# A hybrid block on one core: late gates as a product of seven, sums from raw tiles, and copies and additions issued by GpSimd

## The chip, the cores and the metric

One NeuronCore of a Trainium2 chip runs the whole kernel in one launch. The metric is the device time of one execution in microseconds; the median of several runs counts. The engines: TensorE (PE, its weight loads PEld), VectorE (DVE), ScalarE (ACT), GpSimd (POOL), and SyncE (SP), which only issues DMAs here. Each engine works through its own queue in order; semaphores order engines against each other.

## The reference, cut to what matters

x has 512 tokens of 1024 features. One layer: a projection by w_in to 14,352 columns, a gated delta rule with eight heads (A), a retention with four heads (B), gates that mix both, and an MLP with 4096 hidden features. All is float32.

```python
xn = rmsnorm(x, n_mix_pre)
proj = xn @ w_in
qa, ka, va, za, beta_logit, a_dt, qb, kb, vb, gb, gate_a, gate_b = _split_cols(proj, IN_SIZES)
...
oa = chunk_gated_delta_rule(qa, ka, va, beta, g)
oa = rmsnorm(oa, norm_a) * jax.nn.silu(za.reshape(b, s, A_HEADS, A_DV))
ya = oa.reshape(b, s, A_V) @ w_br_a
...
ob = chunk_retention(qb, kb, vb)
ob = rmsnorm(ob, norm_b.reshape(B_HEADS, B_DV)) * jax.nn.silu(gb.reshape(b, s, B_HEADS, B_DV))
yb = ob.reshape(b, s, B_V) @ w_br_b
mix = (jax.nn.sigmoid(gate_a) * ya + jax.nn.sigmoid(gate_b) * yb) @ w_out
x = x + rmsnorm(mix, n_mix_post)
hn = rmsnorm(x, n_mlp_pre)
ff = jnp.square(jax.nn.relu(hn @ w_up)) @ w_down
return x + rmsnorm(ff, n_mlp_post)
```

The change touches za (2048 columns, four groups of 512 for two heads each, "gates" 0 to 3 below), vb and gb (512 columns per head), gate_a and gate_b (1024 columns each).

## The kernel before, in words

**Products.** Activations and weights are split into a high and a low part, and a product is three matmuls (high by high, high by low, low by high). A weight tile of 128x1024 floats (512 KB) is loaded by SP into one of two `raw` buffers, cast on ACT to `whi` (L145) and subtracted on DVE to `wlo` (L146); both lie in a ring of three. A raw buffer is free for the next load when the subtraction has read it.

**A product of seven.** A product of a 512x1024 activation with 1024 x 1024 weights, cut into 2 x 2 blocks each way, takes eight block products; `seven` does it in seven, from sums of blocks. The sums of the activations ("s1" to "s4") are formed on chip once, in `feature_sums`, after the second recurrence. The sums of the weights are formed in DRAM by `BlockSums`: for each of four sums two DMA copies of 512 KB (`copy`, L165, on SP's queue), and two accumulating DMAs (`add_block`, L132, on GpSimd's queue). These jobs stand in two lists, `trickle` and `later_adds`, and `pace` takes some of them behind each weight load, by a model of the queue (LOAD_US, COPY_US, ADD_US, BACKLOG) that starts at JOBS_FROM. In the two column halves c1, c2 of a unit, `seven` reads three plain blocks from w_in and four sums: 14 raw tiles. `p` and `u` are its sums of finished products.

**Stages.** The first is the delta rule: fillers (products for values `v`, queries `q`, gates `z`, and the products with w_br_a, `ya`) are laid between the steps of chains (inverse, four recurrences for two heads each, gating, transposes) by a model `Clock` that pins TensorE's order. A filler in its list has the events it waits for, such as `og2`, the gated output of heads 4 and 5. A recurrence goes over four chunks of 128 tokens; its steps on TensorE are `kf` (keys by state `st`), `qf`, `rt`, `kd` (the state's update) and `vn,dall` (the output), with short DVE or ACT operations between (L1173, L1189, L1198, L1203). Then come the retention heads and two units of 1024 columns, six uses of `seven` in all (gate a, heads 0 to 3 with vb and gb, gate b), from about 520 to 930 us; then w_out, and the MLP, whose w_down products are products of seven as well (L276 is the matmul of those).

The order of the fillers in the delta stage's last part:

```python
(gate_filler(1), ("gate0",)),
(ya_filler(1), ("og1",)),
(value_filler(3), ("og1",)),
(query_filler(3), ("og1",)),
(gate_filler(2), ("gate1",)),
(ya_filler(2), ("og2",)),
(gate_filler(3), ("gate2",)),
```

The functions that the change touches, with the line numbers of the profile:

Of the kernel before, what the change touches and what calls it, by code (L numbers as in the profile page):

```python
# [19 lines left out]
P = 128  # L20
T = 512
# [7 lines left out]
JOBS_FROM, LOAD_US, COPY_US, ADD_US, BACKLOG = 60.0, 2.0, 2.0, 3.4, 6.0  # L29
SMALL_US, CONV_US, TOK_US, PK_US, INV_US, DB_US = 10.5, 6.5, 2.5, 2.0, 46, 1.2  # L30
VT_US, KS_US, PX_US, PC_US, GATE_US, FEAT_US, INV_PRIO, CONV_PRIO, SMALL_PRIO, KEY_PRIO, DECAY_US, AHEAD, TR_US, REC_PRIO, OUT_PRIO = 2.5, 2.4, 3.5, 2.4, 11.0, 1.0, 0, 600, 800, 600, 20.0, 700, 2.2, 900, 900
# [31 lines left out]
def hybrid_block_kernel(ctx: ExitStack, tc: tile.TileContext, a: dict, out: bass.AP):  # L63
# [32 lines left out]
    def weights(src, k0, nk, c0, ncols, keep=None, paced=True):  # L96
# [9 lines left out]
        pace(load)  # L106
# [5 lines left out]
    def pace(load):  # L112

        if clocks:
            spent[0] = clocks[0].now
        if spent[0] is None:
            return
        queued[0] = max(queued[0], spent[0]) + LOAD_US
        with tc.issue_after(load.ins):
            while (trickle or later_adds) and queued[0] < spent[0] + BACKLOG:  # L120
                ready = len(later_adds) > -(-len(trickle) // 8) * 8
                if ready and (added[0] or not trickle):
                    add_block()
                    queued[0] += ADD_US
                elif trickle:
                    copy_block()
                    queued[0] += COPY_US
                added[0] = not added[0]

    def add_block():  # L130
        dst, src = later_adds.pop(0)
        tc.keep_in_program_order(nc.gpsimd.dma_start(dst, src, accum_op=ALU.add))  # L132
# [19 lines left out]
    class BlockSums:  # L152


        def __init__(self, src, c1, c2, tag):
# [4 lines left out]
            self.t = [dr.tile([P, 4, 512], F32, tag=f"{tag}{i}", name="sums", bufs=1) for i in range(4)]  # L160
            self.parts = []
            trickle.extend((self, i, k) for i in (2, 1, 3, 0) for k in (0, 2))

        def copy(self, i, k):
            nc.sync.dma_start(self.t[i][:, k : k + 2, :], self.first[i][:, k : k + 2, :])  # L165

        def adds(self):

            for i, k in ((2, 0), (1, 0), (3, 0), (2, 2), (1, 2), (3, 2), (0, 0), (0, 2)):
                src = (self.w12, self.t[2], self.w12, self.t[1])[i]  # L170
# [3 lines left out]
        def weights(self, i, ks):  # L174
            while any(job[0] is self for job in trickle):
                copy_block()
            while any(dst is t for dst, src in later_adds for t in self.parts):
                add_block()
            return block_weights(self.t[i - 1][:, 2 * ks : 2 * ks + 2, :])

    def block_weights(block):
# [4 lines left out]
        pace(load)  # L186
        return split_weights(raw, 1024, 2)

    ga_sums = BlockSums(w_in, OFF_GA, OFF_GA + 512, "ga")
    vg_sums = [BlockSums(w_in, OFF_VB + h * 512, OFF_GB + h * 512, f"vg{h}") for h in range(4)]  # L190
    gb_sums = BlockSums(w_in, OFF_GBR, OFF_GBR + 512, "gb")
    down_sums = [BlockSums(w_down[grp * D : (grp + 1) * D, :], 0, 512, f"dn{grp}") for grp in range(3)]
    for sums in [ga_sums] + vg_sums + [gb_sums] + down_sums:
        later_adds.extend(sums.adds())
# [38 lines left out]
    def seven(src, c1, c2, sums, product, temp, out):  # L233

        plain, summed = block_products(src, sums, product)
        p1, u2 = [temp("p1") for _ in range(2)], [temp("u2") for _ in range(2)]
        a = bank(psx)
        plain(a, "11", 0, c1, True)
# [4 lines left out]
        summed(b, "s2", 2, True)  # L243
        with tc.high_priority(400):
            for t in range(2):
                nc.vector.tensor_tensor(u2[t], p1[t], b[t], ALU.add)
        plain(a, "12", 1, c1, False)
        out(0, 0, a)
        c = bank(psm)
        summed(c, "s1", 1, True)  # L250
        summed(b, "s3", 3, False)
        with tc.high_priority(400):
            for t in range(2):
                nc.vector.tensor_tensor(p1[t], p1[t], b[t], ALU.add)
        out(1, 1, c, p1, ALU.subtract)
        d = bank(psx)
        summed(d, "22", 4, True)
        out(1, 0, d, p1, ALU.add)
        plain(c, "s4", 1, c2, False)
        out(0, 1, c, u2, ALU.subtract)  # L260
# [88 lines left out]
    ones = cp.tile([P, P], F32, name="ones")  # L349

# [53 lines left out]
    def two_halves(pool, name, tag, n, width):  # L404
        return Halves(n, [
            pf.tile([P, n, width], F32, tag=tag, name=name),
# [6 lines left out]
    kd = two_halves(pa, "kd", "f1", 16, P)  # L413
# [425 lines left out]

    class Rows:  # L840
# [94 lines left out]
    with delta_rule:  # L935
# [3 lines left out]
        def key_tile(h, ps, th=None):  # L939
# [3 lines left out]
            with tc.high_priority(KEY_PRIO):  # L943
                sum_squares(pt, ssks[h // 4][:, 4 * (h % 4) : 4 * (h % 4) + 4])
                nc.scalar.copy(kd[:, 4 * h : 4 * h + 4, :], pt)
# [210 lines left out]

        def recurrence(g2):
# [4 lines left out]
            for c in range(4):  # L1162
# [28 lines left out]
                if c < 3:  # L1191
                    pc = chain_bank()
                    for hh in range(2):
                        clock.matmul(pc[:, hs[hh], :], kd[:, nn[hh], :], vx[:, hs[hh], :], start=True, stop=True)
# [113 lines left out]
        for step in first_keys_filler():  # L1308
            while any(clock.ready(c[0]) <= clock.now for c in clock.chains):
# [23 lines left out]
                (gate_filler(2), ("gate1",)),  # L1333
                (ya_filler(2), ("og2",)),
                (gate_filler(3), ("gate2",)),
# [7 lines left out]
    with tc.tile_pool(name="pb", bufs=1) as pb_:  # L1343
# [11 lines left out]
        def values_and_gates(sums, c1, c2, g, out1, out2):  # L1355

            def out(th, ch, ps, u=None, op=None):
                for t in range(2):
# [6 lines left out]
                    else:  # L1365
                        nc.vector.tensor_tensor(u[t], ps[t], u[t], op)
                        out1(row, u[t])
# [16 lines left out]
        def scores(h, rows):  # L1384
# [13 lines left out]
            for i in range(4):  # L1398
# [13 lines left out]
                nc.vector.tensor_tensor(sc[:, :n2], ps[:, n - n2 : n], dec[:, :n2], ALU.mult)  # L1412
# [46 lines left out]
        def gate_unit(sums, off, gated):  # L1459

            def out(th, ch, ps, u=None, op=None):
                for t in range(2):
                    src = ps[t]
                    if u is not None:
                        src = tmp("g_s") if th and ch else u[t]
# [38 lines left out]
        def gate_b(t, half, src):  # L1504
            hs = slice(half * 512, half * 512 + 512)
            tb = gates[t // 2][:, t % 2, hs]
            nc.scalar.activation(tb, src, AF.Tanh, scale=0.5)
            m = acc_rows(t, half)
# [12 lines left out]
        for pair in (1, 0):  # L1521
            pss = [[psm.tile([P, T], F32, tag="mm", name="mm") for _ in range(2)] for _ in range(2)]
            for i in range(2):
                t = 2 * pair + i
                tt = slice(t * P, (t + 1) * P)
                for half in range(2):
# [6 lines left out]
                    nc.vector.scalar_tensor_tensor(m, m, 1.0, pss[i][half], ALU.add, ALU.mult)  # L1533
                    nc.vector.tensor_tensor(m, m, acc_rows(t, half), ALU.add)
# [289 lines left out]
```

## Time and profile before

| | |
|---|---|
| median of 3 runs | 1349.88 us (1347.24 to 1351.58) |
| profiled execution | 1347.26 us, span 1345.1 us |
| TensorE busy | 1327.4 us (99%) in 6639 matmuls |
| VectorE, ScalarE, GpSimd busy | 884.8, 634.4, 90.9 us |
| DMA | 236.78 MB, mean 176 GB/s |
| SP's queue (q1), GpSimd's queue (q0) | 43.6%, 19.8% of 16 DMA engines' span |

Line numbers (L146 and so on) are those of the kernel before. "a<-b" is an operation that writes a and reads b; a part in brackets is idle time of the engine just before it, and what ended that. An engine's busy time leaves out the issuing of DMAs on SP, and a load's time runs from its issue to its landing. TensorE's matmuls are pipelined, so a row's duration is longer than the step from one start to the next.

### The profile page before, as it was taken

How to read it: one execution, taken by the hardware profiler on the slowest of the kernel's cores; microseconds unless marked ns; L12 is line 12 of the kernel's file. 1: busy time of each engine (PE TensorE's matmuls, PEld its weight loads, DVE VectorE, ACT ScalarE, POOL GpSimd, SP SyncE). 2: the span in 40 equal slices, each digit the busy share in tenths (PEclk: the TensorE clock that was granted, in tenths of full speed). 3: DMA queues.
4: the chain of work that ended last, by engine and by line, in shares of the span. 5: the costliest groups of instructions: out<-in, count | busy, mean ns of one | idle time of the engine just before them, and what ended most of it. 6: DMA issues, size and time to landing. Idle time of an engine off the chain costs nothing.

```text
span 1345.1 us, 17540 instructions
## 1 busy us (share of the span) xinstructions
PE 1327.4 (99%) x6639; PEld 1101.2 (82%) x6639; DVE 884.8 (66%) x1515; ACT 634.4 (47%) x1118; POOL 90.9 (7%) x99
## 2 busy tenths in 40 slices
PE   9999999999999999999999999999999999999997
PEld 7888778888888877888888888888889888888886
DVE  6889867475476357777467576679684745828535
ACT  5783426553343424553443443455265746346441
POOL 2201110011101010001001000000100000000000
PEclk9999999999999999999999999999999999999999
DMA  6339987489779685899499695565814543535421
GB/s 193 128 95 244 230 191 149 101 227 207 170 187 210 166 227 161 262 309 221 139 278 194 172 258 142 166 206 173 265 67 147 162 146 110 188 98 179 131 78 63
DMA packets 114691, 236.78 MB, mean 176 GB/s; under 512 B 7398, under 2 KB 31120, under 8 KB 114096
## 3 DMA queue, kind: packets, MB, share of 16 engines
q1 hardware_dynamic: 95792, 185.10, 43.6%
q0 software_dynamic: 16496, 43.69, 19.8%
q10 hardware_dynamic: 2320, 6.89, 1.4%
q8 instruction: 52, 0.85, 0.3%
q14 instruction: 31, 0.25, 0.1%
HBM read 231.43 MB, written 79.71 MB: 231 GB/s over the span
## 4 chain that ended last, share of the span: by engine, by line
PE 86%; DVE 6%; ACT 4%; DMA 3%; issue 1%; DVEq 0%; ACTq 0%
PE mm L627 16%; PE mm L276 13%; PE dl L276 12%; PE mm L92 11%; PE mm L93 11%; PE mm L94 11%; PE dl L627 6%; DMA raw<-in_w_in_dram 2%; DVE wlo L146 1%; PE tr L356 1%; PE dl L93 1%; PE dl L94 1%; PE dl L92 1%; PE tr L636 1%; PE mm L591 1%
## 5 line engine op out<-in xcount | busy, mean ns | idle before, releaser
L146 DVE TENSOR_TENSOR wlo<-raw,whi 128x1024 fp32r<-128x1024 f32 x253 | 309.0, 1224 | 243.8 <-ACT whi L145 243.2
L145 ACT CAST whi<-raw 128x1024 fp32r<-128x1024 f32 x253 | 265.9, 1052 | 403.0 <-PE mm L93 100.1
L627 PE MATMUL mm<-actT,whi 128*128 128x512 f32 x448 | 144.3, 403 | 0.0
L276 PE MATMUL mm<-whi,xsum 128*128 128x512 f32 x384 | 121.9, 390 | 0.0
L94 PE MATMUL mm<-hn,wlo 128*128 128x512 f32 (+1 forms) x288 | 105.4, 366 | 0.0
L93 PE MATMUL mm<-hn,whi 128*128 128x512 f32 (+1 forms) x288 | 105.3, 366 | 0.0
L92 PE MATMUL mm<-hn,whi 128*128 128x512 f32 (+1 forms) x288 | 105.3, 366 | 0.0
L627 PEld LDWEIGHTS mm<-actT,whi 128*128 128x128 f32 x448 | 80.6, 188 | 15.1
L276 PE MATMUL dl<-whi,actT 128*128 128x512 f32 x288 | 91.9, 389 | 0.0
L627 PE MATMUL mm<-whi,actT 128*128 128x512 f32 x256 | 87.8, 406 | 1.1 <-DVE qf L857 1.0
L627 PE MATMUL mm<-actT,wlo 128*128 128x512 f32 x224 | 87.8, 392 | 0.0
L276 PEld LDWEIGHTS mm<-whi,xsum 128*128 128x128 f32 x384 | 72.0, 188 | 14.7
L276 PE MATMUL mm<-wlo,xsum 128*128 128x512 f32 x192 | 74.8, 390 | 0.0
L627 PE MATMUL mm<-whi,og 128*128 128x512 f32 x192 | 64.3, 402 | 0.0
L276 PEld LDWEIGHTS dl<-whi,actT 128*128 128x128 f32 x288 | 54.1, 188 | 11.2
L94 PEld LDWEIGHTS mm<-hn,wlo 128*128 128x128 f32 x288 | 54.3, 189 | 8.8
L93 PEld LDWEIGHTS mm<-hn,whi 128*128 128x128 f32 x288 | 54.3, 189 | 8.7
L92 PEld LDWEIGHTS mm<-hn,whi 128*128 128x128 f32 x288 | 54.3, 189 | 8.7
L276 PE MATMUL dl<-whi,ffq 128*128 128x512 f32 x192 | 61.1, 389 | 0.0
L132 POOL DMA_DIRECT2D sums<-sums x36 | 29.9, 830 | 443.2 <-DMA sums<-in_w_in_dram 238.7
L627 PEld LDWEIGHTS mm<-whi,actT 128*128 128x128 f32 x256 | 48.1, 188 | 11.5 <-issue 1.7
L276 PE MATMUL dl<-wlo,actT 128*128 128x512 f32 x144 | 56.0, 389 | 0.0
(372 smaller groups left out, 2789.7 us busy)
## 6 DMA issues: line engine op xcount, KB each, us to landing
raw<-in_w_in_dram SPq DMA_DIRECT2D x97, 512.0 KB, 5.5
raw<-sums SPq DMA_DIRECT2D x72, 512.0 KB, 4.1
sums<-in_w_in_dram SPq DMA_DIRECT2D x48, 512.0 KB, 8.0
sums<-sums POOLq DMA_DIRECT2D x36, 512.0 KB, 7.9
raw<-in_w_up_dram SPq DMA_DIRECT2D x36, 512.0 KB, 4.2
raw<-in_w_down_dram SPq DMA_DIRECT2D x26, 512.0 KB, 3.8
sums<-in_w_in_dram POOLq DMA_DIRECT2D x24, 512.0 KB, 10.8
sums<-in_w_down_dram SPq DMA_DIRECT2D x24, 512.0 KB, 6.9
```

What stands on the lines that cost most here:

```text
L92: nc.tensor.matmul(ps, lh, rh, start=first, stop=False)
L93: nc.tensor.matmul(ps, lh, rl, start=False, stop=False)
L94: nc.tensor.matmul(ps, ll, rh, start=False, stop=last)
L132: tc.keep_in_program_order(nc.gpsimd.dma_start(dst, src, accum_op=ALU.add))
L145: nc.scalar.copy(hi[:, :n], raw[:, :n])
L146: nc.vector.tensor_tensor(lo[:, :n], raw[:, :n], hi[:, :n], ALU.subtract)
L276: m = nc.tensor.matmul(pss[t], lhs[i // 2], rhs[i % 2], start=first and k + i == 0, stop=k + i == 5, skip_group_check=not first,)
L356: nc.tensor.transpose(ps, src, ident)
L591: pin(nc.tensor.matmul(first_keys[f][:, 256:512], ws[w][:, kk, :], xs[x][:, 2 * j + kk, 256:512], start=False, stop=kk == 1 and i == 2, sk ...
L627: m = tc.keep_in_program_order(nc.tensor.matmul(*args, **kwargs))
L636: tc.keep_in_program_order(nc.tensor.transpose(ps, src, ident if by is None else by))
```

## The change

1. `late_gates_filler` takes the place of `gate_filler(2)` and `gate_filler(3)`: gates 2 and 3 (1024 columns of za) are formed by a product of seven, in 14 tiles of 12 matmuls where eight tiles of 24 stood, with a new `z_sums`. It stands where gate 2 stood in the list, so both gates lie ahead of the third w_br_a product and of the last recurrence.
2. In `seven`, two of the four weight sums (the second and the fourth) are no longer made in DRAM but by `plus` on DVE from raw tiles that lie in SBUF. A unit loads ten tiles, adds four times and splits 14 tiles as before; the products come in another order (11, s3, s2, 12, 22, s1, s4), with two more additions to `p` and `u`.
3. The copies for the sums go from SP's queue to GpSimd's. Before it issues jobs, GpSimd copies one element of the weight tile that has just been loaded (`token`), so that it stands behind that landing; then up to two jobs follow, by another pace. JOBS_FROM goes from 60 to 100. There are 56 copies and 56 additions instead of 72 and 72.
4. Smaller things: the keys' token-major tiles `kd` are kept for three chunks instead of four; the decay of the scores gets a higher priority; for half of gate b's rows two DVE operations move behind the product with w_br_b.

The core of the diff:

```diff
-JOBS_FROM, LOAD_US, COPY_US, ADD_US, BACKLOG = 60.0, 2.0, 2.0, 3.4, 6.0
+JOBS_FROM, COPY_US, ADD_US = 100.0, 5.5, 7.5
...
-    def pace(load):
+    def pace(raw):
...
-        queued[0] = max(queued[0], spent[0]) + LOAD_US
-        with tc.issue_after(load.ins):
-            while (trickle or later_adds) and queued[0] < spent[0] + BACKLOG:
-                ready = len(later_adds) > -(-len(trickle) // 8) * 8
...
+        if spent[0] < queued[0] or not (trickle or later_adds):
+            return
+        tc.keep_in_program_order(nc.gpsimd.tensor_copy(token, raw[0:1, 0:1]))
+        done = 0
+        while (trickle or later_adds) and queued[0] <= spent[0] and done < 2:
+            ready = bool(later_adds) and not any(job[0] is later_adds[0][2] for job in trickle)
+            added[0] = ready and (not added[0] or not trickle)
+            if added[0]:
+                add_block()
+            else:
+                copy_block()
+            queued[0] += ADD_US if added[0] else COPY_US
+            done += 1
...
         def copy(self, i, k):
-            nc.sync.dma_start(self.t[i][:, k : k + 2, :], self.first[i][:, k : k + 2, :])
+            tc.keep_in_program_order(
+                nc.gpsimd.dma_start(self.t[i][:, k : k + 2, :], self.first[i][:, k : k + 2, :])
+            )
...
+    z_sums = BlockSums(w_in, OFF_ZA + 1024, OFF_ZA + 1536, "z")
+    ga_sums = BlockSums(w_in, OFF_GA, OFF_GA + 512, "ga", False)
...
     def seven(src, c1, c2, sums, product, temp, out):
...
+        def plus(dst, other):
+            with tc.high_priority(SUM_PRIO):
+                nc.vector.tensor_tensor(dst, other, dst, ALU.add)
...
+        x, y = raws(sums.first_raw, 1), raws(sums.raw, 3)
         a = bank(psx)
-        plain(a, "11", 0, c1, True)
+        times(a, "11", x, True)
...
-        summed(b, "s2", 2, True)
+        x = times(b, "s3", y, True, added(y, x, sums.first_raw, 3))
...
-        plain(a, "12", 1, c1, False)
+        c = bank(psm)
+        times(c, "s2", y, True)
...
+        y = times(a, "12", x, False, added(x, y, sums.raw, 1))
         out(0, 0, a)
-        c = bank(psm)
-        summed(c, "s1", 1, True)
-        summed(b, "s3", 3, False)
...
+        d = bank(psm)
+        x = times(d, "22", x, True, lambda ks: sums.first_raw(2, ks))
+        out(1, 0, d, u3, ALU.add)
+        c = bank(psm)
+        times(c, "s1", y, True)
...
+        def late_gates_filler():
...
+            yield from product(a, "11", None, True)
...
+            yield from product(b, "s2", 2, True)
...
+            yield from product(a, "12", None, False)
+            silu(0, 0, a)
+            yield from product(b, "s3", 3, False)
...
+            yield from product(c, "s1", 1, True)
...
+            yield from product(d, "22", 4, True)
...
+            yield from product(c, "s4", None, False, OFF_ZA + 1536)
...
-                (gate_filler(2), ("gate1",)),
+                (late_gates_filler, ("gate1",)),
                 (ya_filler(2), ("og2",)),
-                (gate_filler(3), ("gate2",)),
```

TensorE's order in the last recurrence before, from the third chunk's `kf` step to its `rt` step (`mm<-whi,actT` and `mm<-wlo,actT` are matmuls of gate 3):

```order
L627 MATMUL dl<-st,kf 128x256 x2
L627 MATMUL dl<-st,qf 128x256 x2
L627 MATMUL mm<-whi,actT 128x512
L627 MATMUL mm<-wlo,actT 128x512
L627 MATMUL mm<-whi,actT 128x512 x2
L627 MATMUL mm<-wlo,actT 128x512
L627 MATMUL mm<-whi,actT 128x512 x2
L627 MATMUL mm<-wlo,actT 128x512
L627 MATMUL mm<-whi,actT 128x512 x2
L627 MATMUL mm<-wlo,actT 128x512
L627 MATMUL mm<-whi,actT 128x512
L627 MATMUL dl<-vt,rt 128x256 x2
```

And now, from the first chunk's `kd` step on (L670 is the matmul of L627; L92 to L94 with `mm<-actT` belong to the next stage's query features):

```order
L670 MATMUL dl<-vt,kd 128x256 x2
L670 MATMUL dl<-vn,dall 128x256 x2
L670 MATMUL dl<-st,kf 128x256 x2
L670 MATMUL dl<-st,qf 128x256 x2
L92 MATMUL mm<-actT,whi 128x512
L93 MATMUL mm<-actT,whi 128x512
L94 MATMUL mm<-actT,wlo 128x512
L670 MATMUL dl<-vt,rt 128x256 x2
L92 MATMUL mm<-actT,whi 128x512
L93 MATMUL mm<-actT,whi 128x512
L94 MATMUL mm<-actT,wlo 128x512
L670 MATMUL dl<-vt,kd 128x256 x2
```

Twelve matmuls of gate 3 stood between two steps of the chain; three matmuls of the next stage stand there now.

DVE's order in a head's unit before (L246 and L254 are the additions to `u` and `p`, L1429 a retention operation):

```order
L146 TENSOR_TENSOR wlo<-raw,whi 128x1024 x7
L246 TENSOR_TENSOR u_5761<-p_5759,mm 128x512
L246 TENSOR_TENSOR u_5762<-p_5760,mm 128x512
L146 TENSOR_TENSOR wlo<-raw,whi 128x1024 x2
L1429 TENSOR_TENSOR vr<-dl,vr 128x512
L146 TENSOR_TENSOR wlo<-raw,whi 128x1024
L1429 TENSOR_TENSOR vr<-dl,vr 128x512
L146 TENSOR_TENSOR wlo<-raw,whi 128x1024 x3
L254 TENSOR_TENSOR p_5759<-p_5759,mm 128x512
L254 TENSOR_TENSOR p_5760<-p_5760,mm 128x512
```

The same unit now (L148 is the split of L146, L258 the addition of two raw tiles, L282 to L288 the additions to `u` and `p`):

```order
L148 TENSOR_TENSOR wlo<-raw,whi 128x1024 x2
L282 TENSOR_TENSOR u_5833<-p_5831,mm 128x512
L282 TENSOR_TENSOR u_5834<-p_5832,mm 128x512
L148 TENSOR_TENSOR wlo<-raw,whi 128x1024
L258 TENSOR_TENSOR raw<-raw 128x1024
L148 TENSOR_TENSOR wlo<-raw,whi 128x1024
L287 TENSOR_TENSOR p_5831<-p_5831,mm 128x512
L288 TENSOR_TENSOR u_5833<-u_5833,mm 128x512
L287 TENSOR_TENSOR p_5832<-p_5832,mm 128x512
L288 TENSOR_TENSOR u_5834<-u_5834,mm 128x512
L258 TENSOR_TENSOR raw<-raw 128x1024
L148 TENSOR_TENSOR wlo<-raw,whi 128x1024 x2
```

Between splits that followed each other, additions of raw tiles stand now, and four additions to `p` and `u` in a row where two stood.

GpSimd's order where the jobs begin, before:

```order
L132 DMA sums<-in_w_in_dram 128x2x512
L132 DMA sums<-sums 128x1024 x2
L132 DMA sums<-in_w_in_dram 128x2x512
L132 DMA sums<-sums 128x1024 x2
L132 DMA sums<-in_w_in_dram 128x2x512 x3
```

And now, a little after the start of the jobs (L120 is the token, L169 a copy, L134 an addition):

```order
L120 COPY token<-raw 1x1
L134 DMA sums<-in_w_in_dram 128x2x512
L120 COPY token<-raw 1x1
L169 DMA sums<-in_w_in_dram 128x2x512
L134 DMA sums<-sums 128x1024
L120 COPY token<-raw 1x1
L169 DMA sums<-in_w_in_dram 128x2x512
L134 DMA sums<-sums 128x1024
```

GpSimd's queue held additions alone; now each group of one or two jobs has a token in front, which waits for the landing of a weight tile and which that tile's buffer waits for.

176 lines of the change are left out of this document (131 added, 45 removed).

## The prediction

> **What bounds the kernel now.** I read the page first, then the stage table, the chain of waits, and TensorE's timeline around its idle places. The page's row of engines, and rows of the stage table (stretch, length, busy time of PE, PEld, DVE, ACT and POOL with their instructions, granted clock, DMA share, GB/s):
>
> ```profile
> PE 1327.4 (99%) x6639; PEld 1101.2 (82%) x6639; DVE 884.8 (66%) x1515; ACT 634.4 (47%) x1118; POOL 90.9 (7%) x99
> 300.00:400.00 100.00, 98.48 (x456) 81.34 (x455) 57.82 (x92) 42.42 (x76) 9.89 (x10) 1.00 0.81 189
> 400.00:480.00 80.00, 79.54 (x372) 65.80 (x371) 41.13 (x78) 32.41 (x73) 9.95 (x10) 1.00 0.79 188
> 480.00:520.00 40.00, 38.36 (x175) 31.02 (x174) 25.99 (x40) 11.13 (x14) 2.82 (x3) 1.00 0.81 210
> 520.00:930.00 410.00, 409.93 (x1865) 339.56 (x1864) 279.66 (x392) 185.31 (x252) 21.86 (x22) 1.00 0.75 210
> sum 1345.10, PE 1327.37 PEld 1101.17 DVE 884.84 ACT 634.37 POOL 90.91; mean PE 110.61 PEld 91.76 DVE 73.74 ACT 52.86 POOL 7.58
> ```
>
> TensorE is the bound: it idles 1345.10 − 1327.37 = 17.7 us in all. Through the retention heads and the gate units around them (520 to 930) it idles 0.07 us in 410; in the last part of the delta stage (300 to 520) 1.52 + 0.46 + 1.64 = 3.6 us. So time is won only by taking matmuls away, or out of those 3.6 us, and is lost wherever another engine or a load makes TensorE wait. The price of a 512-column matmul comes from the chain of waits (start, duration, 24 matmuls):
>
> ```profile
> 529.56 5.44 PE mm L276 x24
> ```
>
> 5.44 / 24 = 0.2267 us.
>
> **The change part by part.**
>
> *Matmuls.* The two late gates are eight weight tiles of 24 matmuls, 192 in all; as a product of seven they are 14 tiles of 12, 168. 24 × 0.2267 = **−5.44 us**, all on the bound. The six other units (gate a, four heads, gate b) were products of seven already; their matmuls only change places.
>
> *The last recurrence without its filler.* Gate 3's 96 matmuls lay between its steps. Now both late gates stand earlier, and this recurrence has six matmuls of the w_br_a product and some fifteen of the next stage's query features to cover its waits. Its steps as TensorE, ACT and DVE ran them, an earlier recurrence standing for some (start, duration, engine, line):
>
> ```profile
> 433.04 1.02 PE L627 MATMUL dl<-vt,rt 128*128 128x256 f32 x4
> 434.10 0.84 ACT L1189 ACTIVATE vt<-dl,brd 128x256 f32<-128x256 f32 x2 [1.17 <-PE dl L627]
> 438.03 1.02 PE L627 MATMUL dl<-vt,kd 128*128 128x256 f32 x4
> 438.89 1.03 PE L627 MATMUL dl<-vn,dall 128*128 128x256 f32 x4
> 439.09 0.69 DVE L1203 COPY st<-dl 128x512 f32<-128x512 f32 x1 [1.22 <-PE dl L627]
> 456.40 1.02 PE L627 MATMUL dl<-st,kf 128*128 128x256 f32 x4
> 457.47 0.88 DVE L1173 SCALAR_TENSOR_TENSOR vt<-dl,neg_eg,vt 128x256 f32<-128x256 f32 x2 [2.84 <-PE dl L627]
> 466.72 1.03 PE L627 MATMUL dl<-vn,dall 128*128 128x256 f32 x4
> 467.39 0.58 PE L92 MATMUL mm<-actT,whi 128*128 128x512 f32 x1
> 467.89 1.13 PE L627 MATMUL dl<-st,kf 128*128 128x256 f32 x4
> ```
>
> The shortest way from one step to the next is from its start to the end of the operation behind it: rt 434.10 + 0.84 − 433.04 = 1.90, kd 1.75 (1.95 where the state update has L1173's 0.88), kf 1.95. A group of four takes TensorE 438.89 − 438.03 = 0.86, so each hop leaves 0.9 to 1.1 us. The new order fills it behind kf with the qf group (0.86), behind kd with the vn,dall group and a matmul (1.09), behind rt with three matmuls (0.68). Short by 0.1, 0 and 0.3 us: four chunks come to about **+1.0**, an estimate. The row of before that is nearest to it is the hop from 466.72 to 467.89, which has the new fillers already: 467.89 − 466.72 − 0.86 − 0.23 = 0.08 idle. Ends: 0, and 4 us (1 us a chunk, where a split stands ahead of a step's copy). Two stalls follow:
>
> ```profile
> 478.69 0.33 PE L636 MATMUL tr<-cmat,vt 128*128 128x128 f32 x1 [0.46 <-DVE vt L1241]
> 511.88 0.50 PE L93 MATMUL dl<-wlo,og 128*128 128x512 f32 x1 [1.44 <-DVE wlo L146]
> ```
>
> Ahead of the transposes at 478.69 stand 26 feature matmuls now, 21 before: 5 × 0.2267 covers the 0.46, **−0.5**. The stall at 511.88 is the first tile of the last w_br_a product. Seven matmuls fewer stand ahead of it (7 × 0.2267 = 1.6), but its loads meet fewer copies: **0**, from −1.4 to +1.6.
>
> *The late gates' supply.* Splits (count, busy us, mean ns), and loads and jobs (count, KB, median us to landing), the first two of 300 to 480, the third of 520 to 930, the rest of the page:
>
> ```profile
> L146 DVE TENSOR_TENSOR wlo<-raw,whi 128x1024 fp32r<-128x1024 f32 x253 | 309.0, 1224 | 243.8 <-ACT whi L145 243.2
> L145 ACT CAST whi<-raw 128x1024 fp32r<-128x1024 f32 x253 | 265.9, 1052 | 403.0 <-PE mm L93 100.1
> raw<-in_w_in_dram SPq DMA_DIRECT2D x16, 512.0 KB, 5.7
> raw<-in_w_br_a_dram SPq DMA_DIRECT2D x10, 512.0 KB, 6.7
> raw<-in_w_br_b_dram SPq DMA_DIRECT2D x16, 512.0 KB, 8.4
> raw<-sums SPq DMA_DIRECT2D x72, 512.0 KB, 4.1
> sums<-in_w_in_dram SPq DMA_DIRECT2D x48, 512.0 KB, 8.0
> sums<-in_w_in_dram POOLq DMA_DIRECT2D x24, 512.0 KB, 10.8
> ```
>
> A raw buffer turns over in landing, cast and subtraction: 4.1 to 5.7, + 1.05 + 1.22 + about 0.2 = 6.6 to 8.2 us for two tiles, as there are two buffers. Two tiles are 2 × 12 × 0.2267 = 5.44 us of gate work, with the chain groups between them some 6.3 to 7.9, an estimate. That is a balance, and up to three split tiles wait in the ring: **0**. Engine time is there: six more splits are 7.3 us on DVE and 6.3 on ACT, which were busy 41.13 and 32.41 of 80.
>
> *The six units' sums on DVE.* A unit loads ten tiles instead of 14 and forms the other four by additions of two raw tiles on DVE: L146's shape, 1.22 us each. One unit before (its stretch of the stage table, and groups in it):
>
> ```profile
> 656.50:694.60 38.10, 38.10 (x169) 31.55 (x169) 24.61 (x27) 19.58 (x23) 1.97 (x2) 1.00 0.81 239
> L146 DVE TENSOR_TENSOR wlo<-raw,whi 128x1024 fp32r<-128x1024 f32 x14 | 17.1, 1225 | 16.5 <-ACT whi L145 16.5
> L254 DVE TENSOR_TENSOR p<-p,mm 128x512 f32<-128x512 f32 x2 | 1.3, 682 | 0.0
> ```
>
> DVE goes from 24.61 to 24.61 + 4 × 1.22 + 4 × 0.68 (two more additions each to p and u) = 32.2 of 38.1 us. It fits as a sum; in a row, additions stand between splits that TensorE needs 2.72 us apart. Laid out in the new order, every tile of a head is split in time, the ninth, behind four additions of p and u, with 0.3 to 0.5 us to spare; in gate b's unit the split behind those four comes about 1 us late. **+1.0**, ends 0 and 7.3 (one split of 1.22 late in each unit).
>
> *Copies, additions, tokens.* 72 copies leave SP's queue and 56 go to GpSimd's; additions fall from 72 to 56. GpSimd copies one element of each landed tile, then issues up to two jobs, and a raw buffer is reused only after that token. Rows of GpSimd, of SP's queue and of ACT's waits (total, times, longest):
>
> ```profile
> L132 POOL DMA_DIRECT2D sums<-sums x36 | 29.9, 830 | 443.2 <-DMA sums<-in_w_in_dram 238.7 <-DMA sums<-in_w_down_dram 132.1 <-DMA sums<-sums 72.5
> POOL sums L132 <- DMA sums<-in_w_in_dram: 331.7, 27, 36.0
> 599.98 0.37 SPq L102 DMA_DIRECT2D raw<-in_w_br_b_dram  x1
> ACT whi L145 <- DMA raw<-in_w_in_dram: 16.2, 4, 5.9
> ```
>
> Issuing costs GpSimd some 112 × 0.83 = 93 us over 800: free. A token's price is in no row; between nothing and an issue's 0.83, beside a turnover of 7 us, it is free too. But an addition waits on GpSimd until its copy has landed, 331.7 / 27 = 12.3 us on average; before, only additions stood behind it, now tokens do, and behind a token SP's next load, the split, TensorE. The pace (5.5 us per copy, 7.5 per addition, additions of a matrix only after its copies) gives most copies a tile or more to land, so I take **0**. What hides a hold is the buffers' turnover, about 7 us; beyond it each costs its excess. Ends: −2.2 (the rest of the 3.6 us of stalls) and +15.9 (below). ACT waited for these loads 16.2 us in all, hidden by split tiles.
>
> [...]
>
> The rest (12 of 16 key tiles kept, scores earlier, two DVE operations of gate b moved behind the product with w_br_b) goes at nothing: DVE is busy 279.66 of 410 us there, and the key tiles that are left out shorten a copy off the path. Without that cover each is worth one DVE operation of 0.68.
>
> *Sum:* −5.44 + 1.0 − 0.5 + 0 + 0 + 1.0 + 0 = −3.9 us. The profiled run took 1347.26 us (span 1345.1), 2.6 below the median of 1349.88, inside the spread of 1347.24 to 1351.58. On the median the forecast is **1346.0**. A measurement of this kernel can tell about 0.3%, 4.05 us, from no change, so the forecast lies on that edge. Its own range: −5.44 − 0.5 − 1.4 = −7.3 to −5.44 + 2 − 0.5 + 1.6 + 2.5 = +0.2, 1342.6 to 1350.1.
>
> **The rivals.**
>
> *The loads gain too (0.15).* 112 jobs instead of 144 move less beside the loads. If all 3.6 us of stalls from 300 to 520 go and nothing is exposed: −5.44 − 3.6 = −9.0, 1340.9. For it: loads land in 6.7 us there, DMA share 0.79 to 0.81. Against: of the two stalls above, one ends on a chain, not on a load.
>
> *The sums come late on DVE (0.10).* One split late in each unit, +7.3 instead of +1.0: +2.4, 1352.3. For it: 0.3 us to spare. Against: 6 of 38 us free.
>
> *GpSimd is held (0.12).* An addition waits for a copy that is not there, tokens queue behind it, and two raw buffers stay taken. It decides above 7 us of hold: an average hold of 12.3 costs 5.3, and two of them put the kernel past 0.3% slower (−3.9 + 10.6 = +6.7). Three: −3.9 + 15.9 = +12, 1361.9. For it: the mean hold of before, and the longest of 36.0. Against: the pace, wider than the 8.0 to 10.8 us in which a job landed.
>
> *The late gates are bound by their loads (0.08).* If loads land in 8.4 us, as w_br_b's did, a turn is 10.9 us against about 7.1 of TensorE work: 7 turns × 3.8 = 26.6, less three split tiles of lead, 10.5: −3.9 + 16 = +12, 1362. Against: loads from the sums landed in 4.1. [...]
>
> **How the numbers follow.** Forecast 0.55, of which 0.33 beyond 0.3% (its range reaches 3.4 us below the edge) and 0.22 within; loads gain 0.15, faster; sums late 0.10, same; the two slower cases 0.20. Faster 0.48, same 0.32, slower 0.20. The range leaves out the slower cases and takes in the others, 1340.5 to 1353.
>
> **What would show it.** In the changed kernel: 24 matmuls fewer; 520 to 930 still without a gap of TensorE, or gaps that end on DVE's wlo (sums late); about 1 us of idle TensorE in the last recurrence; GpSimd's waits for sums under 7 us each, or TensorE gaps behind loads that SP issued late (hold). Wrong would be gaps in the late gates of over 2 us, or raw loads that land later than 6.7 us.

## The result, and the profile after

The changed kernel took 1351.27 us (median of 12 runs, 1345.72 to 1355.05) against 1349.95 us (12 runs, 1346.46 to 1352.48). The ratio is 1.0005, 95% interval 0.9990 to 1.0021: no change that can be measured. The forecast was 1346.0, a ratio of 0.9971, within a range of 1340.5 to 1353; the case that it called likeliest, a gain at the edge of what can be seen, did not come. The profiled execution after took 1350.81 us (span 1349.0), near its median; that of before was one of the faster runs, so the 3.9 us between the two spans are more than the two medians show. About 1.5 of them arise at the very start, before any job is issued: the same ten warm-up matmuls, with no wait between them, took 2.33 us before and 4.45 after, and the first transposes of conv_in start at 34.89 and at 36.43 us. Other runs of kernels with the same start differ as much (34.66 in token_both, 36.38 in early_quiet), so this comes from the run and not from the change:

```profile
5.47 2.33 PE L434 MATMUL warm<-warm 128*128 128x512 bf16 x10
5.56 4.45 PE L477 MATMUL warm<-warm 128*128 128x512 bf16 x10
```

The page's row of engines and rows of the stage table, of the kernel after:

```profile
PE 1328.2 (98%) x6615; PEld 1099.1 (81%) x6615; DVE 935.8 (69%) x1575; ACT 638.0 (47%) x1126; POOL 142.4 (11%) x226
300.00:400.00 100.00, 97.57 (x437) 80.25 (x437) 59.59 (x94) 44.08 (x77) 17.63 (x31) 0.98 0.75 190
400.00:480.00 80.00, 79.66 (x381) 65.15 (x380) 52.20 (x96) 34.95 (x79) 15.95 (x26) 1.00 0.82 176
480.00:520.00 40.00, 36.55 (x157) 29.20 (x156) 23.99 (x35) 10.95 (x14) 7.65 (x11) 0.96 0.84 194
520.00:930.00 410.00, 407.50 (x1848) 336.41 (x1847) 313.43 (x430) 181.16 (x248) 53.12 (x88) 1.00 0.69 179
```

TensorE has 24 matmuls less (6615 against 6639), as said. But its idle time rose from 17.7 to 1349.0 − 1328.2 = 20.8 us, and its busy time did not fall: in two stages the granted clock (the third number from the end) is below 1.00, where it was 1.00 before. From 300 to 520 it idles 2.4 + 0.3 + 3.5 = 6.2 us (3.6 before), from 520 to 930 2.5 (0.07 before).

The costliest of the new stalls is in the late gates. The chain of waits through it (start, duration, what), and the rows of GpSimd, ACT and TensorE around it:

```profile
323.27 8.94 DMA raw<-sums
332.31 1.04 ACT whi L147
333.36 0.38 ACT vt L1311
333.78 3.05 PE dl L670 x8
...
321.39 1.16 POOL L134 DMA_DIRECT2D sums<-in_w_in_dram  x1 [0.28 <-issue]
332.31 1.04 ACT L147 CAST whi<-raw 128x1024 fp32r<-128x1024 f32 x1 [7.58 <-DMA raw<-sums]
333.78 1.34 PE L670 MATMUL dl<-vt,kd 128*128 128x256 f32 x4 [2.43 <-ACT vt L1311]
```

At 320.9 a tile has landed, the token releases GpSimd, and an addition is issued at 321.39. The next load waits for the split of that tile and is issued at 323.27, behind the addition. It lands 8.94 us later. ACT's queue has the cast of this load ahead of the recurrence's scaling (`vt`, L1311), so a recurrence that needs nothing of the load waits as well, and TensorE behind it 2.43 us. Then TensorE runs on a slower clock (stage table in steps of 3.41 us, granted clock third from the end):

```profile
331.15:334.56 3.41, 0.98 (x5) 0.69 (x5) 1.17 (x1) 2.25 (x5) 1.86 (x3) 1.00 0.23 59
334.57:337.98 3.41, 3.41 (x10) 2.64 (x9) 1.74 (x3) 2.17 (x4) 0.74 (x2) 0.50 0.81 238
```

0.50 × 3.41 = 1.7 us more; the eight matmuls of the chain from 333.78 on took 3.05 us, the eight from 340.20 on 1.73. The second place is the rotary table's load, with two jobs issued beside it (the load's row is that of 480 to 520, median us to landing):

```profile
487.29 1.16 POOL L134 DMA_DIRECT2D sums<-in_w_in_dram  x1 [0.28 <-issue]
488.00 1.16 POOL L169 DMA_DIRECT2D sums<-in_w_down_dram  x1
rope<-in_c_rope_dram ACTq DMA_DIRECT2D x1, 512.0 KB, 11.3
498.79 0.69 DVE L1496 TENSOR_TENSOR ro<-mm,rope 128x512 f32<-128x512 f32 x1 [8.83 <-DMA rope<-in_c_rope_dram]
500.13 0.50 PE L92 MATMUL mm<-whi,og 128*128 128x512 f32 x1 [1.75 <-DVE ro L1497]
510.79 0.50 PE L93 MATMUL dl<-wlo,og 128*128 128x512 f32 x1 [1.43 <-DVE wlo L148]
```

Before, this table landed at the same time (498.6 against 498.7) and cost TensorE nothing, since TensorE came to it later: it is what was late next. The 1.43 at 510.79 is the old stall of 511.88, now with 1.7 us of slower clock behind it. The third place is the first head's output, where a cast that waits for a load again stands ahead of work that does not need it (`osq`, L1572):

```profile
603.23 1.05 ACT L147 CAST whi<-raw 128x1024 fp32r<-128x1024 f32 x1 [3.96 <-DMA raw<-in_w_in_dram]
605.95 0.50 PE L92 MATMUL dl<-vr,s 128*128 128x512 f32 x1 [1.02 <-ACT osq L1572]
```

### The profile page after: what moved, and what is told of

It is laid out like the page before. It is cut to its first block, busy times and chain, and to the rows that moved or that the text cites. A ratio compares the mean times of both kernels' runs of the same rounds, so it can differ in the third digit from the quotient of the medians.

```text
span 1349.0 us, 17650 instructions
## 1 busy us (share of the span) xinstructions
PE 1328.2 (98%) x6615; PEld 1099.1 (81%) x6615; DVE 935.8 (69%) x1575; ACT 638.0 (47%) x1126; POOL 142.4 (11%) x226
## 4 chain that ended last, share of the span: by engine, by line
PE 83%; DVE 7%; DMA 4%; ACT 4%; issue 1%; ACTq 0%; DVEq 0%; SPq 0%
PE mm L670 18%; PE mm L318 12%; PE mm L92 11%; PE mm L93 11%; PE mm L94 11%; PE dl L318 8%; PE dl L670 6%; DMA raw<-in_w_in_dram 2%; DVE wlo L148 2%; PE tr L399 1%; PE dl L92 1%; PE dl L93 1%; PE dl L94 1%; PE tr L679 1%; DMA raw<-sums 1%
## 5 line engine op out<-in xcount | busy, mean ns | idle before, releaser
L147 ACT CAST whi<-raw 128x1024 fp32r<-128x1024 f32 x259 | 272.0, 1052 | 416.1 <-PE mm L93 95.5
L148 DVE TENSOR_TENSOR wlo<-raw,whi 128x1024 fp32r<-128x1024 f32 x259 | 315.8, 1223 | 218.0 <-ACT whi L147 215.7
L670 PE MATMUL mm<-actT,whi 128*128 128x512 f32 x448 | 144.3, 403 | 0.0
L94 PE MATMUL mm<-hn,wlo 128*128 128x512 f32 (+1 forms) x288 | 105.4, 366 | 0.0
L92 PE MATMUL mm<-hn,whi 128*128 128x512 f32 (+1 forms) x288 | 105.3, 366 | 0.0
L670 PEld LDWEIGHTS mm<-actT,whi 128*128 128x128 f32 x448 | 80.5, 188 | 14.9
L120 POOL COPY token<-raw 1x1 f32<-1x1 f32 x87 | 32.9, 378 | 519.5 <-DMA raw<-in_w_in_dram 346.8
L670 PE MATMUL mm<-actT,wlo 128*128 128x512 f32 x224 | 87.7, 392 | 0.0
L670 PE MATMUL mm<-whi,og 128*128 128x512 f32 x192 | 62.4, 397 | 0.0
L94 PEld LDWEIGHTS mm<-hn,wlo 128*128 128x128 f32 x288 | 54.3, 189 | 8.8
L670 PE MATMUL mm<-whi,actT 128*128 128x512 f32 x176 | 60.4, 405 | 1.0 <-DVE qf L908 1.0
L92 PEld LDWEIGHTS mm<-hn,whi 128*128 128x128 f32 x288 | 54.3, 189 | 8.7
L318 PE MATMUL dl<-whi,actT 128*128 128x512 f32 x192 | 61.1, 389 | 0.0
L1787 DVE TENSOR_TENSOR ffq<-r,ffq 128x512 fp32r<-128x512 f32 (+2 forms) x51 | 33.8, 678 | 29.1 <-ACT ffq L1787 29.0
L92 PE MATMUL mm<-actT,whi 128*128 128x512 f32 x128 | 51.5, 402 | 0.0
L94 PE MATMUL mm<-actT,wlo 128*128 128x512 f32 x128 | 50.8, 397 | 0.0
```

The lines of the kernel that those rows point to most:

```text
L92: nc.tensor.matmul(ps, lh, rh, start=first, stop=False)
L94: nc.tensor.matmul(ps, ll, rh, start=False, stop=last)
L120: tc.keep_in_program_order(nc.gpsimd.tensor_copy(token, raw[0:1, 0:1]))
L147: nc.scalar.copy(hi[:, :n], raw[:, :n])
L148: nc.vector.tensor_tensor(lo[:, :n], raw[:, :n], hi[:, :n], ALU.subtract)
L318: m = nc.tensor.matmul(pss[t], lhs[i // 2], rhs[i % 2], start=first and k + i == 0, stop=k + i == 5, skip_group_check=not first,)
```

## The experiments

Twelve kernels, each timed in five rounds against the kernel before on the same chip. The chips differ between rows, so the ratios are to be compared, not the medians. The second theory, formed from the trace: **A**, the jobs' DMAs make loads late, above all because a job is issued at the moment at which a tile lands and so ahead of the next load; ACT's queue carries the delay to work that needs no load. Its rivals: **B**, two raw buffers cannot feed the late gates; **C**, tokens that GpSimd reads late hold the raw buffers; **D**, the sums on DVE lose the time.

| kernel | ratio to before (95%) | median, us |
|---|---|---|
| changed kernel | 1.0005 (0.9990 to 1.0021) | 1351.27 |
| nojobs_before | 0.9960 (0.9948 to 0.9972) | 1342.66 |
| nojobs_after | 0.9921 (0.9909 to 0.9933) | 1337.39 |
| quiet_gates | 1.0020 (1.0001 to 1.0038) | 1349.99 |
| token_split | 0.9982 (0.9967 to 0.9997) | 1345.50 |
| token_cast | 1.0036 (1.0023 to 1.0049) | 1351.82 |
| token_both | 1.0095 (1.0082 to 1.0108) | 1359.94 |
| old_gates | 1.0009 (0.9993 to 1.0026) | 1349.57 |
| sp_copies | 1.0000 (0.9987 to 1.0014) | 1347.88 |
| gates_only | 1.0025 (1.0007 to 1.0044) | 1349.75 |
| split_quiet | 0.9998 (0.9986 to 1.0010) | 1347.49 |
| early_jobs | 1.0170 (1.0147 to 1.0192) | 1372.17 |
| early_quiet | 1.0049 (1.0035 to 1.0062) | 1354.59 |

**Without jobs: what the rest of the change is worth.**

```diff
+    trickle.clear()          # no copies; later_adds stays empty: no additions
-            return block_raw(self.t[i - 1][:, 2 * ks : 2 * ks + 2, :])
+            return block_raw(self.first[i - 1][:, 2 * ks : 2 * ks + 2, :])
```

> The changed kernel without its 112 copies and additions and without tokens: the loads of sums read a plain block of the weights instead, so the output is not the reference's, and every product, split and DVE sum stays, in the same order on TensorE. If the jobs' DMAs make the late loads: the stalls in the late gates, at the rotary load and before the heads' outputs go, what stays is about 1 us in the last recurrence and 1 us in gate b's unit, and the time is 8 to 10 us below the changed kernel, ratio 0.993 to 0.995. If the new order on ACT and DVE makes the stalls: ratio 0.998 to 1.000.

> The kernel before without its 144 jobs, loads of sums from a plain block (output not the reference's). Its TensorE idles little beside jobs already: 1 to 4 us below before, ratio 0.997 to 0.999. The distance to the run before this one is then what matmuls and DVE sums alone give: about 4 us, the forecast's term. If before is held by its jobs as much as the changed kernel: ratio 0.993 to 0.995, and the distance is 0 to 1 us.

Measured 0.9921 and 0.9960: the change without jobs gains 1342.66 − 1337.39 = 5.3 us, the 24 matmuls nearly whole. The jobs cost the kernel before 0.0040 × 1348.4 = 5.4 us (by the interval, 1.6 more or less), more than expected. With their tokens they cost the changed kernel 1.0005 − 0.9921 = 0.0084, 11.3 us (2.6 more or less), though it has 112 of them and not 144. The five runs of each also lie within 0.4 and 1.2 us of each other, where twelve of before and of after spread over 6 and 9, which points to the jobs for that spread too. Where the 5.3 us come from is read from starts of the same instruction, first without jobs before, then after (PE's timeline; in order the last `rt` of the third recurrence, the last transposes of the gated output, the outputs of heads 0 and 3, and the first transposes behind gate b):

```profile
367.19 1.02 PE L626 MATMUL dl<-vt,rt 128*128 128x256 f32 x4
486.27 0.60 PE L635 MATMUL tr<-cmat,vt 128*128 128x128 f32 x4
595.24 0.39 PE L92 MATMUL dl<-vr,s 128*128 128x512 f32 x1
878.10 0.39 PE L92 MATMUL dl<-vr,s 128*128 128x512 f32 x1
981.26 0.60 PE L355 MATMUL tr<-cmat,fw 128*128 128x128 f32 x4
```

```profile
366.36 1.02 PE L669 MATMUL dl<-vt,rt 128*128 128x256 f32 x4
480.16 0.60 PE L678 MATMUL tr<-cmat,vt 128*128 128x128 f32 x4
588.51 0.39 PE L92 MATMUL dl<-vr,s 128*128 128x512 f32 x1
871.32 0.39 PE L92 MATMUL dl<-vr,s 128*128 128x512 f32 x1
975.85 0.60 PE L398 MATMUL tr<-cmat,fw 128*128 128x128 f32 x4
```

The differences are −0.83, −6.11, −6.73, −6.78 and −5.41: up to the first, where both have run equally many matmuls, 0.8 us of earlier idle time is gone; from there to the transposes TensorE has 21 matmuls less (4.8 us) and 0.4 us less idle time, together −5.28; the other three matmuls are gone on the way to head 0 (−0.6); the four heads give nothing, and gate b takes 1.4 back. B and D fall: without jobs two raw buffers feed the late gates (from 315 to 340 a load landed in 3.4 us, in the median), and the DVE sums cost nothing outside gate b. Loads from 520 to 930, and ACT's waits for such loads over the whole run, first of the changed kernel, then without jobs:

```profile
raw<-in_w_in_dram SPq DMA_DIRECT2D x46, 512.0 KB, 6.6
ACT whi L147 <- DMA raw<-in_w_in_dram: 40.0, 14, 5.3
```

```profile
raw<-in_w_in_dram SPq DMA_DIRECT2D x66, 512.0 KB, 4.0
ACT whi L147 <- DMA raw<-in_w_in_dram: 8.6, 3, 4.7
```

**When a job is issued.** Three kernels move the token; token_split reads what DVE's subtraction writes, when the next load can go too, token_cast what ACT's cast writes, a step earlier, and token_both reads the raw tile and then the split one.

```diff
-        pace(raw)
...
             nc.vector.tensor_tensor(lo[:, :n], raw[:, :n], hi[:, :n], ALU.subtract)
+        pace(lo)          # token_cast: pace(hi)
...
+        hold(raw)         # token_both alone: one more token, of the raw tile
```

> The changed kernel with the token read from the low part that DVE writes in the split, not from the raw tile: jobs come one split later, beside or behind the next load, and no raw buffer waits for GpSimd. Theory A: loads land earlier (w_in tiles from 520 to 930 in 5 to 5.5 us instead of 6.6), ACT's waits for raw tiles fall from 56 us to below 25, no stall in the late gates; ratio about 0.996 to 0.998. Rival C (the raw buffers held by tokens delay the loads): the same time, but then the next kernel is as slow as the changed one. Rival B: ratio 1.000 or more.

> The changed kernel with the token read from the high part that ACT's cast writes: GpSimd no longer holds a raw buffer, but jobs still come before the next load, which waits for DVE's subtraction one step later. If the order of job and load is what counts (theory A): like the changed kernel, ratio 1.000 to 1.002. If the hold of the raw buffers counts (C): like token_split, ratio 0.997 to 0.9985.

> As the kernel before this one, but GpSimd also reads the raw tile as in the changed kernel, so that raw buffers wait for GpSimd while the jobs still come behind the split. Theory A: like token_split, within 1.5 us. Rival C: like the changed kernel, ratio 1.000 to 1.002.

token_split came out at 0.9982, some 3 us below the changed kernel, and is the only kernel with its jobs in it that lies below both; the gain is at the edge of what can be seen (its interval ends at 0.9997, that of the changed kernel begins at 0.9990). token_cast holds no raw buffer either; it reads the other half of the same split, so that its jobs come before the next load, and it was 0.0054 slower. By the traces the median job was issued 0.6 us behind the last load in token_split, and ahead of the next one by 1.0 us in token_cast and by 2.7 us in the changed kernel. So the order of job and load counts, and freeing the raw buffers alone does not help (C falls for the changed kernel). That token_cast is also slower than the changed kernel (1.0036 against 1.0005) was not expected and stays open.

Theory A's signs came only in part. In token_split the late gates have no stall, and ACT waited 34 us for w_in tiles and sums instead of 56 (below 25 was expected). But the w_in tiles from 520 to 930 landed in 6.4 us, hardly sooner than 6.6, the rotary table took 12.0 us, and TensorE waited 2.40 us for it. The order of issue accounts for some 3 of the jobs' 11.3 us; the rest stayed in every placing that was tried.

token_both has its jobs where token_split has them (0.5 us behind a load) and came out at 1.0095, so C is real as a mechanism: there a raw tile's token stands behind the split of the tile before it. SP's waits for tokens (total, times, longest), of the changed kernel and of token_both:

```profile
SPq L102 <- POOL token L120: 5.6, 4, 4.0
SPq L102 <- POOL token L127: 16.7, 46, 2.7
```

Theory A's number for token_both was wrong by some 13 us.

**Undoing parts.** old_gates puts the two gate fillers back. sp_copies takes pace and copies of before (SP's queue, no tokens), with the changed kernel's rule that a matrix is copied before it is added to; gates_only takes the old `seven` as well, with four sums in DRAM and 160 jobs (the smaller things of the change stay in it).

```diff
 # old_gates
-                (late_gates_filler, ("gate1",)),
+                (gate_filler(2), ("gate1",)),
                 (ya_filler(2), ("og2",)),
+                (gate_filler(3), ("gate2",)),
 # sp_copies, gates_only
-                nc.gpsimd.dma_start(self.t[i][:, k : k + 2, :], self.first[i][:, k : k + 2, :])
+            nc.sync.dma_start(self.t[i][:, k : k + 2, :], self.first[i][:, k : k + 2, :])
```

> The changed kernel with gates 2 and 3 as before (eight tiles of 24 matmuls, gate 3 between the steps of the last recurrence, 16 jobs fewer). Theory A: 5.44 us of matmuls come back, the stalls of the late gates (4.4 us at their first tiles) and of the last recurrence (about 2) go: within 2 us of the changed kernel, ratio 1.000 to 1.002; gaps in the six units stay. Rival D (the six units' sums on DVE lose all): ratio above 1.003.

> The changed kernel with copies on SP's queue behind each load, the start at 60 us and the pace of before, no tokens; late gates and DVE sums as changed. A and C both expect the loads to land as before (w_in 5.4 us from 520 to 930) and the stall in the late gates to go: ratio 0.996 to 0.998. If the DVE sums or the late gates lose the time themselves: 1.000 or more, with gaps before wlo.

> Before with the late gates alone: the old seven with four sums in DRAM, copies on SP, 160 jobs instead of 144. The 24 matmuls bring 5.44 us, the last recurrence and the stall at the rotary load take 1 to 3 back: ratio 0.997 to 0.9985. If 16 more jobs make the loads late (DMA bound): 1.000 or more.

All three came out at before or above it: 1.0009, 1.0000, 1.0025. The late gates alone gain nothing beside 160 jobs; the copies' move to GpSimd, with the new pace, neither makes nor removes the loss; and without the late gates the changed kernel is no slower than with them. Only old_gates was expected so. In sp_copies the loads from 520 to 930 landed in 4.7 us, but stalls stood in the late gates, from 354 us on, and at the inverse, from 144, in a stretch (100 to 150) in which 19 jobs were issued by its timelines where the changed kernel has 7:

```profile
145.54 1.07 PE L666 MATMUL dl<-rn,acc 32*32 32x32 f32 x32 [1.73 <-DVE rn L1068]
357.23 1.13 PE L666 MATMUL dl<-st,kf 128*128 128x256 f32 x4 [3.23 <-ACT vt L1326]
```

**Moving the jobs.** quiet_gates lets no job go during the late gates; split_quiet is token_split without jobs around the rotary load; early_jobs is token_split with an earlier start and a faster pace, and early_quiet both.

```diff
+        if quiet[0]:
+            queued[0] = spent[0]
+            return
...
-JOBS_FROM, COPY_US, ADD_US = 100.0, 5.5, 7.5
+JOBS_FROM, COPY_US, ADD_US = 20.0, 4.5, 6.0
```

> The changed kernel without any copy, addition or token while the late gates run (the jobs move behind them; nothing is left out). Theory A (a job is issued the moment a tile lands and so stands ahead of the next load on the DMA engines; the late load then holds ACT's queue): the 2.43 us stall in the late gates goes, the granted clock is 1.00 from 300 to 400 instead of 0.98, and the time is 3 to 5 us below the changed kernel, ratio to before about 0.997. Rival B (two raw buffers cannot feed tiles of 12 matmuls, jobs or not): a stall of over 1 us stays in the late gates, ratio about 1.000 to 1.001.

> token_split, and no jobs from the second half of the third w_br_a product until the last one is under way, so that the load of the rotary table (512 KB, 11.4 us to landing in the changed kernel) meets no job. If the jobs make that load late: it lands in 5 to 7 us, the 2.4 us stall of TensorE before the last w_br_a product goes, clock 1.00 from 480 to 520, and the time is 3 to 4 us below token_split: ratio 0.995 to 0.9965. If its place in the queue or the release of its buffer is what counts: the stall stays, ratio as token_split's 0.998.

> token_split with the jobs begun at 20 us instead of 100, at 4.5 and 6.0 us instead of 5.5 and 7.5, so that they end near 610 us instead of 830: the last three heads and gate b meet none, the stages before meet more. If a job costs most where a unit's or a gate's loads follow each other every 2.7 us: ratio 0.995 to 0.997. If jobs cost the same wherever they lie: as token_split, 0.998; a stall at 145 us (inverse) would come back.

> As early_jobs, and no jobs around the rotary load (from the second half of the third w_br_a product until the last one is under way). The rotary table lands in 5 to 7 us and its stall of 2.4 us with the slower clock behind it goes, and the delayed jobs end by about 650 us, before the last heads: 2 to 4 us below early_jobs. If the delayed jobs only move the stalls, as in split_quiet: no gain over early_jobs, with a stall of over 2 us near 595.

In quiet_gates the late gates ran without a stall, at full clock, as expected, but the 3 to 5 us did not come: new stalls stood later, at the output of head 0 and in gate b, beside whose loads jobs were issued (in gate b they had ended in the changed kernel; first the stage row, then the two new stalls):

```profile
300.00:400.00 100.00, 100.00 (x460) 83.33 (x459) 63.83 (x97) 47.08 (x80) 10.12 (x17) 1.00 0.58 161
599.52 0.50 PE L92 MATMUL dl<-vr,s 128*128 128x512 f32 x1 [4.49 <-ACT osq L1577]
920.88 1.03 PE L402 MATMUL tr<-cmat,o 128*128 128x128 f32 x4 [2.59 <-DVE og L387]
```

split_quiet did the same at the rotary load, which landed in 6.7 us instead of token_split's 12.0 and cost no stall. Again the gain did not come: TensorE waited 3.33 us at head 0's output (599.47), and in gate b, where token_split had no jobs left, a load met one (ACT's row, then TensorE's):

```profile
917.03 1.05 ACT L149 CAST whi<-raw 128x1024 fp32r<-128x1024 f32 x1 [4.63 <-DMA raw<-sums]
920.74 1.09 PE L401 MATMUL tr<-cmat,o 128*128 128x128 f32 x4 [3.05 <-DVE og L386]
```

early_jobs, expected to gain, lost 23 us to before, and here the rival of the prediction, that GpSimd is held, is seen at work (rows of GpSimd, DVE and TensorE):

```profile
548.82 0.87 POOL L133 DMA_DIRECT2D sums<-sums  x1 [11.01 <-DMA sums<-in_w_down_dram]
549.76 1.22 DVE L147 TENSOR_TENSOR wlo<-raw,whi 128x1024 fp32r<-128x1024 f32 x1 [2.61 <-POOL token L119]
551.04 0.79 PE L317 MATMUL mm<-wlo,actT 128*128 128x512 f32 x1 [2.45 <-DVE wlo L147]
```

An addition waited 11.01 us for its copy, the token behind it was read late, the ring's tile stayed taken, DVE's split waited, and TensorE. It is the only wait of DVE for a token in this trace, so it is a small part of the 23 us; the others were not taken apart. early_quiet, with the same pace and a pause, lost 7 us, 16 less than early_jobs where 2 to 4 were expected; why is open.

## Why the prediction was right or wrong

Its range held, and its chances gave 0.32 to what came; its likeliest case did not come. Step by step:

- **Matmuls, −5.44.** Right: 21 and 3 matmuls are missing where they should be, and the two kernels without jobs are 5.3 us apart, with what other terms give and take.
- **The last recurrence without its filler, +1.0 − 0.5.** Both terms were mis-sized. Of the +1.0 nothing came: from 400 to 480 TensorE idles 0.34 us, all of it ahead of the transposes, and there 0.46 stood before, so −0.1 came and not −0.5. A hop was priced up to the end of a whole row of ACT or DVE, 1.90 us for `rt`. Without jobs the last `kd` starts 1.59 us behind its `rt` (457.30 and 458.89), while ACT's row runs until 459.20: the next step does not wait for all of it. The working was also off in itself: four chunks short by 0.1, 0 and 0.3 come to 1.6, not 1.0.
- **The stall at 511.88, 0 (−1.4 to +1.6).** It is the jobs' work: without them neither kernel has it. With them it stayed (1.43), now with 1.7 us of slower clock behind it, and a new one of 1.75 us stood ahead of it, at the rotary load. The prediction asked what covers this stall, but not what would be late next if TensorE came earlier: the rotary load had landed only just in time before.
- **The six units' sums on DVE, +1.0.** Right: without jobs nothing in the four heads, 1.4 in gate b, where it was put. The rival of late sums did not come.
- **Copies, additions, tokens: 0 (−2.2 to +15.9).** This is the step that failed: +5.9 (11.3 after against 5.4 before, some 3 us more or less). A sign that the prediction named for being wrong, a gap of over 2 us in the late gates, came with it. The prediction priced the jobs by GpSimd's issue time and by what a hold would cost, and took the loads' landing of 5.4 to 5.7 us as given. But that landing is itself what the jobs make of 3.5 to 4.0 us, as the kernels without jobs show. An issue from GpSimd right at a landing puts the job ahead of the next load (2.7 us in the median), and the split tiles in the ring cover TensorE's weights only, not what stands in ACT's queue behind a cast that waits for its load: the recurrence, or a head's output (2.43 and 1.02 us of TensorE's waiting). This order is only part of the +5.9. sp_copies, with its copies behind the loads on SP's queue and no tokens, still lies 1.0000 − 0.9921 = 0.0079 above the changed kernel without jobs, 10.7 us. Why fewer jobs cost the changed kernel about twice what they cost the one before, in either order, stays open.
- **GpSimd held (0.12).** Not what happened here, though holds of over 7 us, its mark, came: all nine, of 7 to 15 us, fell after 608, when four raw buffers are in use instead of two, and TensorE had no stall of over 0.5 us there up to the end of gate b. With a faster pace one cost TensorE 2.45 us (early_jobs).
- **Loads bound the late gates (0.08).** At one tile, by the price that was given for it, a landing of 8 to 9 us; not as a stage.
- **The copies' move off SP's queue, 0.** What it is worth alone no run shows. sp_copies, with its 56 copies back on SP's queue, the pace of before and no tokens, gave 1.0000, no measurable difference to 1.0005.
- **A token's price, between nothing and an issue's 0.83 us.** The 87 tokens took 0.17 to 1.43 us, 0.28 in the median. One of 1.07, from 333.58 on, stands beside a subtraction that runs until 334.62. No wait of TensorE ends on it.

```profile
332.33 0.17 POOL L120 COPY token<-raw 1x1 f32<-1x1 f32 x1 [9.78 <-DMA raw<-sums]
333.39 1.23 DVE L148 TENSOR_TENSOR wlo<-raw,whi 128x1024 fp32r<-128x1024 f32 x1 [7.26 <-ACT whi L147]
333.58 1.07 POOL L120 COPY token<-raw 1x1 f32<-1x1 f32 x1
```

## What to carry to other kernels

Price background DMAs by what they add to the landing of the loads beside them (here a median of 6.6 us against 4.0 for w_in's from 520 to 930), not by what their issue costs (0.83 us); the quickest way to that price is a run without them. Try to issue them behind the next load, not at the landing of the last one; here that was worth some 3 us against the changed kernel and 7 against token_cast, of the jobs' 11. And where one engine's queue mixes work that waits for loads with work that a chain waits for, a late load can stall the chain: here a cast waited 7.58 us for its load, and TensorE 2.43 us for the scaling behind that cast. Taking such a stall away in one place did not pay where the DMAs that caused it met the next tight load (in quiet_gates new waits of 4.49 and 2.59 us).

## What the runs showed of the hardware

A stall of TensorE can cost nearly as much again behind it: the 2.43 us of waiting that end at 333.78 were followed by 3.41 us at a granted clock of 0.50, which lost 1.7 us. It is not a matter of the stall's length alone. In sp_copies a stall of 1.73 us before 145.54 was followed by 6.83 us at 0.50, one of 3.23 us before 357.23 by none (rows of the stage table, in this order):

```profile
144.03:147.44 3.41, 1.90 (x36) 1.76 (x37) 3.36 (x4) 1.23 (x2) 0.00 (x0) 1.00 0.89 156
147.44:154.27 6.83, 6.83 (x66) 4.97 (x65) 4.76 (x10) 6.07 (x10) 5.79 (x7) 0.50 0.91 202
352.24:355.65 3.41, 1.77 (x8) 1.13 (x6) 0.55 (x2) 0.26 (x1) 1.14 (x1) 1.00 0.77 256
355.65:359.07 3.42, 1.84 (x9) 1.63 (x10) 1.86 (x3) 3.39 (x10) 0.00 (x0) 1.00 0.88 130
359.07:362.48 3.41, 3.41 (x17) 2.81 (x16) 3.02 (x5) 1.52 (x3) 0.00 (x0) 1.00 0.72 187
```

The rows follow a grid that the traces give themselves. In the changed kernel the clock is low twice between the warm-up and the last 5 us, for 3.413 us from 334.57 and from 512.06 on: 177.49 = 52 × 3.413. The 6.83 us of sp_copies are two steps of this length. The stall of 3.23 us lies across an edge of the grid, with 1.64 and 1.58 us of idle time on its two sides.

The idle time in one stretch of the grid does not settle it in these runs either. Behind 2.43 us (331.15 in the changed kernel), 1.64 us (508.65) and 1.51 us (144.03 in sp_copies) the clock was 0.50; behind 1.73 us (498.41 in the changed kernel) and the 1.64 us of sp_copies (352.24) it stayed at 1.00. The other stretches of the changed kernel, from 20 us to 1341, have 1.02 us or less, and the clock stays at 1.00 behind them; in the kernel before the most is 1.44 us (510.31), up to 1336, and there too it stays at 1.00. Two of these stretches with the one behind each, of the changed kernel:

```profile
498.41:501.82 3.41, 1.69 (x7) 1.42 (x8) 3.03 (x6) 0.00 (x0) 0.00 (x0) 1.00 1.09 353
501.82:505.23 3.41, 3.41 (x16) 2.82 (x16) 3.41 (x6) 0.00 (x0) 0.00 (x0) 1.00 0.48 174
508.65:512.06 3.41, 1.77 (x7) 1.23 (x7) 3.41 (x5) 1.61 (x3) 1.04 (x1) 1.00 0.81 120
512.06:515.47 3.41, 3.41 (x10) 2.67 (x9) 3.33 (x6) 0.62 (x1) 0.00 (x0) 0.50 1.13 206
```

That a stall's place on the grid decides is the author's estimate from these rows and not shown: no run here moved one stall on purpose.
